# 96 free bytes behind the operand tile `tl`, and a DMA scratch of 1 KB, in a two-layer decoder trunk

## The chip, the core and the metric

The kernel runs on one core of one Trainium2 chip. The metric is the device time of one execution in microseconds. Besides TensorE (PE in the profile, its weight loads PEld) it uses VectorE (DVE), ScalarE (ACT), a little GpSimd (POOL), and SyncE (SP), whose queue issues all DMAs. On-chip memory (SBUF) is spoken of by a tile's address within one partition; all 128 partitions hold the same layout.

## What is computed

The reference is a decoder trunk of two layers over 256 tokens of width 1024, in float32, cut here to its frame:

```python
for layer in range(DEPTH):                       # DEPTH = 2
    x = x + mixer_block(rms_norm(x, nm), wi, wa, wb, wo)
    h = rms_norm(x, nf)
    x = x + (swiglu(h, *fp) if layer % 2 == 0 else moe_swiglu(h, *fp))
return rms_norm(x, norm_final)
```

`mixer_block` projects the 1024 columns to 5888 (queries, keys and values of two attentions, two gates), runs the attentions, projects each branch back to 1024, gates and adds them, and applies an output projection. `swiglu` is `(silu(h @ w_gate) * (h @ w_up)) @ w_down` with an inner width of 2816. `moe_swiglu` does the same with 8 experts of inner width 3584, two experts per token. The weights come to 429 blocks of 1 MiB.

## The kernel before

**Weights.** A `Stream` (lines 119 to 167) loads the weights in blocks of 128 x 2048 float32 into a ring of tiles: `raw0` to `raw3`, later also `ringa0` to `ringa5`, `ringb0` to `ringb3` and, once each, `late0` and `late1`. SP issues the load of a block when the block that lay in its slot has been split. Half a block at a time (128 x 1024) is split into two float32r parts: ACT copies it to a tile `wh` (line 152), DVE subtracts that from the original and writes a tile `wl` (line 153). `take()` keeps the split `AHEAD = 4` halves in front of the products, and `wh` and `wl` have five buffers each.

**Products.** Activations too are kept as two float32r parts, transposed, with 1024 rows spread over 128 partitions. `th` and `tl` hold the two parts of the normalised input of each stage (and of the merged branches ahead of the output projection); in the expert stage they hold the gathered tokens of an expert. `gTh` and `gTl` hold the inner activations of the dense channel mixer, `gT` and `tmp` those of the experts (two buffers that take turns; `tmp` also holds an expert's weighted result), and `oAh`, `oAl`, `oBh`, `oBl` the outputs of the two attentions. `run` (lines 250 to 260) multiplies: the activation part is the stationary operand (128 x 128, so 512 bytes of each partition), the weight part the moving operand (up to 512 columns, 2048 bytes of each partition). Three products make one: high by high (line 254), low by high (line 255), then high by low of the weights (line 259):

```python
for b, o in enumerate(outs):
    T.matmul(o, xh(b), wh, start=start, stop=False)
    T.matmul(o, xl(b), wh, start=False, stop=False)
...
    T.matmul(o, xh(b), wl, start=False, stop=stop)
```

In the first three stages (mixer, dense channel mixer, mixer) there are two outputs of 128 tokens, so half a block gives 12 products; in the experts there is one output, and half a block gives 6.

**Order.** The order of all work is written out by hand. `soon` and `later` put side work (transposes, softmax, gathers, scatters) between the products at distances counted in products, by `tick`. Each engine runs its instructions in that order and waits on semaphores.

**Where tiles lie.** Pools take SBUF in the order in which they are opened. At address 0 lies a scratch area for DMA descriptors, 16384 bytes unless the program says otherwise; the tiles of the pool `base` follow in the order of the code, each rounded up to 32 bytes: `xs`, `C`, `CB`, the four `raw`, `th`, `tl`, then `ss`, `ms`, `rstd`, `nhalf`, `base_e` (five of 32 bytes), `junk` (1024), `wrhl` (512) and `zeros` (256). Behind `base` lies the pool `hp` with `wh` and `wl`, and behind that the pools of the stages. Pools with `side="right"` (the attentions' work tiles, `ringa`) grow from the other end. `th` and `tl` (lines 210 and 211) start at 256 modulo 512, and the small tiles behind them shift all that follows by 416, so `wh`, `wl` and the tiles of the stages start at 160 modulo 512.

Of the kernel before, what the change touches and what calls it, by code (L numbers as in the profile page):

```python
# [11 lines left out]
F32 = mybir.dt.float32  # L12
# [3 lines left out]
AF = mybir.ActivationFunctionType  # L16
# [3 lines left out]
P = 128  # L20
# [15 lines left out]

# distances of the steps of the attention, the norms and the experts, in us of the weights' products
PAR = dict(a_step=4.02, a_e=1.5, a_n=4.0, a_t=8.7, a_v=11.7, a_act_n=0, a_act_t=1,
# [3 lines left out]

# [1 line left out]

# [59 lines left out]

# [1 line left out]
C_ID = 0  # L106
# [12 lines left out]
class Stream:  # L119
    """Weights in blocks of 1 MiB: loaded into a ring, then split exactly into two float32r parts, half a block at a time."""  # L120

# [49 lines left out]
def trunk(ctx: ExitStack, tc: tile.TileContext, x, xt, wpre, wmoe, cst, cstb, gfin, out):  # L171
    nc = tc.nc
# [18 lines left out]

# [1 line left out]
    xs = base.tile([P, 2, D], F32, name="xs")  # L193
# [16 lines left out]
    th = base.tile([P, 8, S], F32R, name="th")  # L210
    tl = base.tile([P, 8, S], F32R, name="tl")
    ss = base.tile([P, 2, 2], F32, name="ss")
    ms = base.tile([P, 2], F32, name="ms")
# [6 lines left out]

# [1 line left out]
    urgent, side = [], []  # L222
# [27 lines left out]
    def run(blocks):  # L250
        """Products with both parts of a block of weights: [(w_hi, w_lo, x_hi, x_lo, outs, start, stop)]."""
        for wh, wl, xh, xl, outs, start, stop in blocks:
            for b, o in enumerate(outs):
                T.matmul(o, xh(b), wh, start=start, stop=False)  # L254
                T.matmul(o, xl(b), wh, start=False, stop=False)  # L255
            tick(len(outs) * wh.shape[-1] / 1200)
        for wh, wl, xh, xl, outs, start, stop in blocks:
            for b, o in enumerate(outs):
                T.matmul(o, xh(b), wl, start=False, stop=stop)  # L259
            tick(len(outs) * wh.shape[-1] / 2400)  # L260
# [4 lines left out]
    def half(xT, outs, k0, nk, width, first, last):  # L265
        """Half a block of weights: row blocks k0.. of one chunk of columns."""
        h, l = W.take()
        r = []
        for i in range(nk):
            o = i * width  # L270
            r.append((h[:, o:o + width], l[:, o:o + width], col(xT[0], k0 + i), col(xT[1], k0 + i),
                      [p[:, 0:width] for p in outs], first and i == 0, last and i == nk - 1))
        run(r)
# [6 lines left out]
    def chunk(outs, xT=(th, tl), c=512, first=False):  # L280
        """One chunk of columns of a product over 1024 rows: two blocks of 512 columns, or one of 256."""
        if c == 512:
            unit(xT, outs, 0, 4, 512, True, False)
            if first:
                flush()
            unit(xT, outs, 4, 4, 512, False, True)
        else:
            unit(xT, outs, 0, 8, 256, True, True)

# [1 line left out]
    def gain(gi, k):  # L291
# [21 lines left out]
    def norm_half(gi, c):  # L313
        at = PAR['xt0'] if c == 0 else PAR['xt1']
        if gi == 3 and c == 1:
            # the router waits for it
            sumsq(xs, c)
        soon(at, lambda: x_transpose(gi, 2 * c))
        soon(at + 0.8, lambda: x_transpose(gi, 2 * c + 1))
        if gi != 3 or c == 0:  # L320
            soon(at + 1, lambda: sumsq(xs, c))
# [13 lines left out]

# [1 line left out]
    def mixer(i, gnext, last=False):  # L337
# [26 lines left out]
    def attention(mp, ap):  # L364
# [34 lines left out]
        def qk(src, kofs, pair, kind, mx):  # L399
            """Masked scores of two heads, in SBUF, with their row maxima."""  # L400
            s = [acc_ps(), acc_ps()]
            for b, (c0, c1) in enumerate(HALVES):
                for i in range(2):
                    h = slice(i * HD, (i + 1) * HD)
                    T.matmul(s[i][:, c0:c1], src[h, pair, b * P:(b + 1) * P], src[h, kofs + pair, 0:c1 - c0],
                             start=True, stop=True)
            prs = []
            for i in range(2):
                pr = ap.tile([P, 384], F32, name="pr", tag="pr", bufs=12)
                for b, (c0, c1) in enumerate(HALVES):  # L410
                    V.tensor_tensor_reduce(pr[:, c0:c1], s[i][:, c0:c1], mask[:, kind * 384 + c0:kind * 384 + c1],
                                           1.0, -3.0e38, ALU.add, ALU.max, mx[:, i, b:b + 1])
                prs.append(pr)
            return prs
# [24 lines left out]
        def weigh(items, dst, pair):  # L439
            """Weighted values, transposed: [(row offset of the head, transposed weights, values)]."""  # L440
            o = tp_ps()
            tot = len(items) // 2
            for n, (r, pt, v) in enumerate(items):
                T.matmul(o[r:r + HD, 0:S], v[:, 0, :], pt[:, 0:256], start=n < 2, stop=False,
                         skip_group_check=True)
            for n, (r, pt, v) in enumerate(items):
                T.matmul(o[r:r + HD, P:S], v[:, 1, :], pt[:, 256:384], start=False, stop=n // 2 == tot - 1,
                         skip_group_check=True)
            split_ps(dst[0][:, pair, :], dst[1][:, pair, :], o[:, 0:S])
# [78 lines left out]

        # queries and keys of A
        o = pair_ps()  # L530
# [9 lines left out]
        rope_chunk(o, qkA, 4)  # L540
        # values of A
        o = pair_ps()
# [4 lines left out]
        queue_A(PAR['a_step'])  # L547
        # queries and keys of B
        for c in range(3):
            o = pair_ps()  # L550
            chunk(o)
            rope_chunk(o, qkB, 4 * c)
        # values of B
        o = pair_ps()
# [8 lines left out]
        queue_B()  # L563
        # gates
        gates = []
# [14 lines left out]

    # projections of the branches, gated and summed
    def projections(mp, attended):
# [40 lines left out]

# [1 line left out]
    def ffn(gnext):  # L625
# [41 lines left out]

# [1 line left out]
    def more_slots(n, **kw):  # L669
# [8 lines left out]
    def moe_open():  # L678
        A.activation(junk[:, 0:2], nhalf, AF.Silu)     # its table, ahead of the experts
        ep = M["ep"] = ctx.enter_context(tc.tile_pool(name="moe", bufs=2, reuse_waits="tile"))  # L680
        # tiles of the experts' later steps, until then room for one more block each
        late = [ep.tile([P, UNIT], F32, name=f"late{i}", tag=f"late{i}", bufs=1) for i in range(2)]
        M["late"] = late
        W.add_slots(late, once=True)
        M["xo"] = late[1].rearrange("p (b d) -> p b d", b=2)
        M["gT"] = [ep.tile([P, 2, 4, P], F32R, name="gT", bufs=1)]
        more_slots(RING_MOE - RING_ATT, name="ringb")

    def logits(c):
        """The router's products with four of the eight row blocks."""  # L690
        if c == 0:
# [7 lines left out]
    def route():  # L699
# [16 lines left out]
        for b in range(2):  # L716
            V.scalar_tensor_tensor(L[:, b, :], lp[b][:, 0:8], rstd[:, b:b + 1], lo[:, b, :],
                                   op0=ALU.mult, op1=ALU.add)
        # rank by value, then by index
        lt = C[:, C_LT:C_LT + 64].rearrange("p (e j) -> p e j", e=8).unsqueeze(1).to_broadcast([P, 2, 8, 8])  # L720
# [8 lines left out]
        for b in range(2):  # L729
            V.tensor_copy(rc[:, b, :, 0], rstd[:, b:b + 1].to_broadcast([P, 8]))  # L730
        # slots are counted from 1, 0 where the expert is not chosen
        pp = mm_ps()
# [9 lines left out]
        def weights():  # L742
# [4 lines left out]
            for b in range(2):  # L747
                V.max(v8[:, b, :], L[:, b, :])
            # softmax of the two chosen: 1 / (1 + e^(m1 + m2 - 2 l))
            for b in range(2):  # L750
# [11 lines left out]
    def expert_prep(e, off):  # L762
        """The tokens of an expert's slots off..off+127: selection, gathered operand, their scales."""
        ep, par = M["ep"], e % 2
# [136 lines left out]
    def warm(n):  # L901
        """Products that nobody reads: they keep the tensor engine's clock up while it waits."""
        p = mm_ps()
# [40 lines left out]

# [1 line left out]
    most = nc.values_load(M["most"][0:1, 0:1], min_val=0, max_val=S)  # L946
# [6 lines left out]

# [1 line left out]
    xo = M["xo"]  # L955
# [9 lines left out]

# [1 line left out]
def constants(inputs):  # L967
# [60 lines left out]
```

## Time and profile before

| what | us |
|---|---|
| three timed runs | 1637.98, 1638.15, 1639.14 |
| their median | 1638.15 |
| the profiled execution, first to last instruction (its span) | 1637.1 |
| PE busy in it | 1620.4 |
| DVE busy | 1296.4 |
| ACT busy | 1096.2 |

The profiled execution has no separate time beside its span; the span lies 1.05 us below the median of the three runs.

The profile comes from one execution. A busy share says how long an engine had an instruction in work, not that it went at its best rate: products on PE are pipelined, their recorded durations overlap, and how fast they follow each other is read from the distance between their starts. The view of instructions in order of time gives these starts; the view of groups gives counts, busy time, mean duration and the idle time ahead of a group with what ended it. The stages by time: first mixer to 203 us, dense channel mixer to about 400 us, second mixer to 603 us, routing to about 615 us, experts to 1627 us, final norm.

### The profile page before, as it was taken

The page shows a single profiled execution, that of the slowest core. Times are in us where ns is not written, and L with a number is a line of the kernel's source. Part 1 is how long each engine was busy: PE and PEld are TensorE (multiplying, and loading weights), DVE is VectorE, ACT ScalarE, POOL GpSimd, SP SyncE. Part 2 cuts the span into 40 slices and gives each one's busy share as a digit, 9 for nine tenths or more (in the row PEclk, how much of TensorE's full clock was granted, in tenths as well). Part 3 has the DMA queues.
Part 4 walks back from the last instruction along what each step waited for, and adds up shares of the span by engine and source line. Part 5 has one row for each costly group of instructions (what it writes and reads, how often), then busy time and mean ns, then how long its engine had stood idle before and what let it go on. Part 6 is the DMA issues. An engine that isn't in the chain of part 4 may idle for free. (4 is left out here: it accounts for less than half of the span.)

```text
span 1637.1 us, 21105 instructions
## 1 busy us (share of the span) xinstructions
PE 1620.4 (99%) x7661; PEld 1308.2 (80%) x7661; DVE 1296.4 (79%) x1654; ACT 1096.2 (67%) x1413; POOL 6.6 (0%) x10
## 2 busy tenths in 40 slices
PE   9999999999999999999999999999999999999996
PEld 6777888888777778888888888888888888888885
DVE  7767655555776668899899889889889899889996
ACT  6556454445556447777777777777777777777774
POOL 0000000000000000000000000000000000000000
PEclk9999999999999999999999999999999999999998
DMA  8444545455444596899899999999999899989960
GB/s 328 163 146 139 179 171 188 176 189 203 165 144 147 215 385 232 332 362 348 334 358 360 335 361 346 337 365 346 333 374 346 335 362 357 356 327 369 349 255 28
DMA packets 64305, 456.17 MB, mean 279 GB/s; under 512 B 7104, under 2 KB 7360, under 8 KB 9408
## 3 DMA queue, kind: packets, MB, share of 16 engines
q1 hardware_dynamic: 64192, 454.73, 74.3%
q8 instruction: 62, 1.02, 0.2%
q14 instruction: 51, 0.42, 0.1%
HBM read 453.66 MB, written 1.05 MB: 278 GB/s over the span
## 5 line engine op out<-in xcount | busy, mean ns | idle before, releaser
L254 PE MATMUL mm<-wh,th 128*128 128x512 f32 (+1 forms) x1536 | 611.4, 400 | 2.0 <-ACT wh L152 2.0
L255 PE MATMUL mm<-wh,tl 128*128 128x512 f32 (+1 forms) x1536 | 599.1, 392 | 0.0
L153 DVE TENSOR_TENSOR wl<-raw,wh 128x1024 fp32r<-128x1024 f32 x376 | 448.3, 1220 | 142.1 <-ACT wh L152 141.2
L152 ACT ACTIVATE wh<-raw 128x1024 fp32r<-128x1024 f32 x376 | 390.9, 1058 | 154.6 <-PE mm L255 118.4
L259 PE MATMUL mm<-wl,th 128*128 128x512 f32 (+1 forms) x1536 | 459.2, 395 | 0.0
L153 DVE TENSOR_TENSOR wl<-ringa,wh 128x1024 fp32r<-128x1024 f32 x290 | 341.6, 1220 | 30.4 <-ACT wh L152 28.9
L254 PEld LDWEIGHTS mm<-wh,th 128*128 128x128 f32 x1536 | 289.9, 189 | 70.6 <-issue 5.0
L255 PEld LDWEIGHTS mm<-wh,tl 128*128 128x128 f32 x1536 | 290.2, 189 | 61.5
L259 PEld LDWEIGHTS mm<-wl,th 128*128 128x128 f32 x1536 | 281.5, 188 | 64.1 <-issue 2.0
L152 ACT ACTIVATE wh<-ringa 128x1024 fp32r<-128x1024 f32 x290 | 298.4, 1058 | 40.9 <-PE mm L255 24.4
L153 DVE TENSOR_TENSOR wl<-ringb,wh 128x1024 fp32r<-128x1024 f32 x188 | 219.0, 1220 | 21.5 <-ACT wh L152 21.4
L152 ACT ACTIVATE wh<-ringb 128x1024 fp32r<-128x1024 f32 x188 | 192.9, 1061 | 27.2 <-PE mm L255 12.7
L255 PE MATMUL acc<-wh,gT 128*128 128x512 f32 x224 | 87.5, 391 | 0.0
L254 PE MATMUL acc<-wh,gT 128*128 128x512 f32 x224 | 87.5, 391 | 0.0
L255 PE MATMUL acc<-wh,tmp 128*128 128x512 f32 x224 | 87.5, 391 | 0.0
L254 PE MATMUL acc<-wh,tmp 128*128 128x512 f32 x224 | 87.4, 390 | 0.0
L259 PE MATMUL acc<-wl,gT 128*128 128x512 f32 x224 | 69.2, 390 | 0.0
L259 PE MATMUL acc<-wl,tmp 128*128 128x512 f32 x224 | 69.2, 390 | 0.0
L865 ACT ACTIVATE g<-mm,sc 128x512 f32<-128x512 f32 x56 | 38.7, 692 | 42.2 <-PE mm L259 42.2
L254 PEld LDWEIGHTS acc<-wh,tmp 128*128 128x128 f32 x224 | 42.1, 188 | 9.0
L254 PEld LDWEIGHTS acc<-wh,gT 128*128 128x128 f32 x224 | 42.1, 188 | 9.0
L255 PEld LDWEIGHTS acc<-wh,gT 128*128 128x128 f32 x224 | 42.0, 188 | 9.1
(178 smaller groups left out, 1260.0 us busy)
## 6 DMA issues: line engine op xcount, KB each, us to landing
ringa<-in_wmoe_dram SPq DMA_DIRECT2D x144, 1024.0 KB, 6.7
raw<-in_wmoe_dram SPq DMA_DIRECT2D x96, 1024.0 KB, 6.4
ringb<-in_wmoe_dram SPq DMA_DIRECT2D x94, 1024.0 KB, 6.7
raw<-in_wpre_dram SPq DMA_DIRECT2D x91, 1024.0 KB, 4.8
late<-in_wmoe_dram SPq DMA_DIRECT2D x2, 1024.0 KB, 7.9
raw<-in_wpre_dram SPq DMA_DIRECT2D x2, 512.0 KB, 6.3
xs<-in_x_dram SPq DMA_DIRECT2D x2, 512.0 KB, 6.4
ringa<-in_wpre_dram SPq DMA_DIRECT2D x1, 1024.0 KB, 7.0
```

The source lines that it names most:

```text
L152: self.nc.scalar.activation(h, s, AF.Copy)
L153: self.nc.vector.tensor_tensor(l, s, h.bitcast(F32), op=ALU.subtract)
L254: T.matmul(o, xh(b), wh, start=start, stop=False)
L255: T.matmul(o, xl(b), wh, start=False, stop=False)
L259: T.matmul(o, xh(b), wl, start=False, stop=stop)
L865: A.activation(g, og, AF.Silu, scale=sl["sc"][:, 0:1])
```

## The change

96 bytes are taken in the pool `base` behind `tl`, by a tile `gap` that nothing reads or writes, and the program is built with a DMA scratch of 1024 bytes in place of 16384. The diff also drops comments, which is left out here.

```diff
     th = base.tile([P, 8, S], F32R, name="th")
     tl = base.tile([P, 8, S], F32R, name="tl")
+
+    base.tile([P, 24], F32, name="gap")
     ss = base.tile([P, 2, 2], F32, name="ss")
...
-    nc = bacc.Bacc("TRN2", target_bir_lowering=False, num_devices=1)
+    nc = bacc.Bacc("TRN2", target_bir_lowering=False, num_devices=1, dynamic_dma_scratch_size=1024)
```

In the built programs the instructions of every engine stand in the same order with the same waits; nothing but addresses differs. The scratch moves all tiles on the left side down by 15360 bytes, which is 30 times 512. The start addresses modulo 512:

| tiles | before | after |
|---|---|---|
| `th`, `tl` | 256 | 256 |
| `wh`, `wl` (all ten buffers) | 160 | 256 |
| `gTh`, `gTl`, `gT`, `tmp`, `oAh`, `oAl`, `oBh`, `oBl` | 160 | 256 |
| `raw0` to `raw3` | 256 | 256 |
| `ringa0` to `ringa5` | 480 | 480 |
| `ringb0` to `ringb3` | 384 | 480 |
| `late0`, `late1` | 160 | 256 |
| `xs`, the identity in `C` | 128 | 128 |
| `G` (selection of an expert's tokens) | 352 | 448 |
| `GT` (the same, transposed) | 384 | 480 |
| `g` in the dense stage, in the experts | 160, 320 | 256, 416 |
| `merged0`, `merged1`, `t1`, `qkA`, `vA`, gates | 160 | 256 |
| `pr`, `pt`, `qkB`, `vB` | 96 | 96 |

The rows of `th` and of the other operand tiles are multiples of 512 bytes long, so each stationary operand starts at its tile's place modulo 512, and each moving operand of 512 columns too.

## Rows read from the trace of the kernel before

**Rows 1.** The page: span; busy us of each engine; granted TensorE clock in 40 slices.
```profile
span 1637.1 us, 21105 instructions
...
PE 1620.4 (99%) x7661; PEld 1308.2 (80%) x7661; DVE 1296.4 (79%) x1654; ACT 1096.2 (67%) x1413; POOL 6.6 (0%) x10
...
PEclk9999999999999999999999999999999999999998
```

**Rows 2.** Waits of PE, longest first: waiting, releaser, us, times, longest us.
```profile
PE mm L254 <- ACT wh L152: 2.0, 2, 1.7
```

**Rows 3.** Groups by shape: line, engine, operation, names, shapes, count, busy us, mean ns.
```profile
L254 PE MATMUL mm<-wh,th 128*128 128x512 f32 x1472 | 595.9, 405 | 2.0 <-ACT wh L152 2.0
L255 PE MATMUL mm<-wh,tl 128*128 128x512 f32 x1472 | 583.6, 396 | 0.0
L259 PE MATMUL mm<-wl,th 128*128 128x512 f32 x1472 | 450.1, 399 | 0.0
...
L255 PE MATMUL acc<-wh,gT 128*128 128x512 f32 x224 | 87.5, 391 | 0.0
...
L255 PE MATMUL mm<-wh,gTl 128*128 128x512 f32 x88 | 34.3, 390 | 0.0
...
L254 PE MATMUL mm<-wh,th 128*128 128x256 f32 x64 | 15.6, 282 | 0.0
...
L255 PE MATMUL mm<-wh,oAl 128*128 128x512 f32 x32 | 12.5, 391 | 0.0
```

**Rows 4.** PE in order of time, dense stage, gate products: start us, us, instruction.
```profile
253.72 0.40 PE L254 MATMUL mm<-wh,th 128*128 128x512 f32 x1
...
262.16 0.60 PE L632 MATMUL tp<-C,g 128*128 128x128 f32 x4
```

**Rows 5.** The same view, dense stage, down projection.
```profile
375.64 0.40 PE L254 MATMUL mm<-wh,gTh 128*128 128x512 f32 x1
...
383.81 0.39 PE L254 MATMUL mm<-wh,gTh 128*128 128x512 f32 x1
```

**Rows 6.** The same view, first mixer, output projection.
```profile
194.92 0.39 PE L254 MATMUL mm<-wh,th 128*128 128x512 f32 x1
...
200.54 0.39 PE L254 MATMUL mm<-wh,th 128*128 128x512 f32 x1
```

**Rows 7.** The same view, experts: an up chunk, then the down projection.
```profile
1030.94 0.39 PE L254 MATMUL mm<-wh,th 128*128 128x512 f32 x1
...
1036.55 0.39 PE L254 MATMUL acc<-wh,gT 128*128 128x512 f32 x1
...
1042.02 0.60 PE L882 MATMUL tp<-C,g 128*128 128x128 f32 x4
1042.38 0.48 PE L254 MATMUL mm<-wh,th 128*128 128x512 f32 x1
1042.70 0.40 PE L255 MATMUL mm<-wh,tl 128*128 128x512 f32 x1
```

**Rows 8.** Busy us in stretches of 50 us; at the end clock, DMA share, GB/s.
```profile
1000.00:1050.00 50.00, 49.98 (x231) 40.73 (x230) 46.12 (x47) 37.28 (x43) 0.00 (x0) 1.00 0.96 352
```

**Rows 9.** Instructions writing `wl`: duration ns min/median/max, first and last start us.
```profile
L153 DVE TENSOR_TENSOR wl<-raw,wh x376: 1210/1219/1228, 7.2 to 1607.9; 128x1024 fp32r<-128x1024 f32 x188
...
L153 DVE TENSOR_TENSOR wl<-late,wh x4: 1217/1218/1219, 642.0 to 645.4; 128x1024 fp32r<-128x1024 f32 x4
```

**Rows 10.** DMA: GB/s in 40 slices, queues, issues with us to landing.
```profile
GB/s 328 163 146 139 179 171 188 176 189 203 165 144 147 215 385 232 332 362 348 334 358 360 335 361 346 337 365 346 333 374 346 335 362 357 356 327 369 349 255 28
...
q1 hardware_dynamic: 64192, 454.73, 74.3%
...
ringa<-in_wmoe_dram SPq DMA_DIRECT2D x144, 1024.0 KB, 6.7
...
ringb<-in_wmoe_dram SPq DMA_DIRECT2D x94, 1024.0 KB, 6.7
```

**Rows 11.** Waits of the SP queue: waiting, releaser, us, times, longest us.
```profile
SPq L142 <- DVE wl L153: 1289.7, 392, 19.3
```

## The prediction, made before the changed kernel ran

> **What bounds the kernel now.** [...] Then the waits: the longest wait of PE in total is 2.0 us, for ACT's `wh` [rows 2]. So PE never waits for a feeder, and what PE's instructions take one behind the other is the time. DVE is busy 46.12 of 50 us in a stretch of the experts, second to PE but with 3.9 us to spare [rows 8]; SP's queue spends 1289.7 us waiting for DVE to free a ring slot [rows 11], so the loads wait for the products and not the other way round.
>
> A busy share of 99% doesn't say that the products go at their best rate. So the third view is PE in order of time, and there the distance between starts. The dense stage gives two stretches of 36 products, three half blocks of 12, with no other instruction between them:
> - gate products, `th` and `tl` stationary: from 253.72 to 262.16 us, 8.44 us, 234.4 ns each [rows 4];
> - down projection, `gTh` and `gTl` stationary: from 375.64 to 383.81 us, 8.17 us, 226.9 ns each [rows 5].
>
> Same shapes, types, moving tiles and PSUM tiles (`mm`), and a difference of 7.5 ns. The experts show it back to back: 24 products with `th` from 1030.94 to 1036.55 us, 233.8 ns each, then 24 with `gT` to 1042.02 us, 227.9 ns each [rows 7]. The mean durations agree: 396 to 405 ns with `th` and `tl`, 390 or 391 ns with `gT`, `gTl` and `oAl` [rows 3]. It isn't the data: in the output projection `th` holds the merged branches instead of a norm's output, and 24 products from 194.92 to 200.54 us take 234.2 ns each [rows 6]. Nor is it the stage, since each of them holds both kinds. What the 234 ns products have in common, and none of the 227 ns products shares, is the place: `th` and `tl` start at 256 modulo 512 and meet weights at 160, while `gT`, `gTl`, `oAl` and their kin start at 160, as the weights do.
>
> **The change, part by part.** No instruction is added, removed or moved, and no wait. What changes is where `wh` and `wl` lie: at 256, the place of `th` and `tl`. The other stationary tiles go along to 256, so every product with weights then has both operands at one place, as the 227 ns products have today.
>
> *The products with `th` and `tl`.* There are 3 x 1472 = 4416 of 512 columns [rows 3]. In the experts they are 8 experts x 14 chunks x 8 row blocks x 3 = 2688, so 1728 lie in the first three stages. I take for each kind the difference in its own stage: 1728 x 7.5 ns = 13.0 us, and 2688 x (233.8 - 227.9 = 5.9 ns) = 15.9 us. Together 28.9 us. All of this is on the path, since PE waits for nothing. By the smaller difference for all it is 26.1 us, by the larger 33.1 us.
>
> *The 192 products of 256 columns* (3 x 64 [rows 3]) have no counterpart at one place in the trace. Between nothing and half of the 7.5 ns each they are worth 0 to 0.7 us; I take 0.3, as half the columns stream by.
>
> *Products just behind other work on PE.* Behind transposes the first product takes 0.32 us to the next start [rows 7], 85 ns above the usual, because its weights can't be loaded ahead. Such a product may gain nothing. By the order in the code there are some 200 (each group of transposes, gathers or scores makes one), so 0 to 1.5 us of the 28.9 would fail to come; I take 0.8.
>
> *The products with the other stationary tiles* number 3 x (224 + 224 + 88 + 32 + 16) = 1752, for `gT`, `tmp`, `gTh`, `oAh` and `oBh` (three of these counts, or those of the twin product, stand in [rows 3]). Both their operands move by 96 together. If only the distance between them matters, they stay at 227 to 228 ns. If the place itself matters they could go to 234 ns, 7.5 x 1752 = 13.1 us lost at the most, or win something that no row prices. I take 0: the nearest rows are these products themselves, at an unchanged distance.
>
> *Small products.* Transposes take 0.60 us for four with the source at 160 (`g` of the dense stage [rows 4]) and 0.60 us with it at 320 (`g` of the experts [rows 7]) against the same identity, so places don't show there. The gathers, scores and weighted values, some 500 products of 128 to 256 columns, change their distances too; at a quarter of 7.5 ns each way that is 1 us up or down. I take 0.
>
> *ACT and DVE* read and write the same tiles at new places: `wl`, `wh` and `raw` then lie at one place. The four splits from `late` already have that, all three at 160, and take 1218 ns against 1219 ns where `raw` lies 96 away [rows 9]. No price, and it is off the path by the margin above.
>
> *DMA.* `ringb` goes from 384 to 480, where `ringa` is; both land 6.7 us behind their issue [rows 10]. The smaller scratch has no reader: all loads go through the hardware queue, 64192 packets [rows 10], and POOL issues none. If it delayed a load after all, the loads wait on free slots far ahead of the products [rows 11]. The products will ask for more: 15.9 us less in the experts' 985 us is 1.6%, some 358 GB/s in place of 352 [rows 8], while a slice of 41 us ran at 385 [rows 10].
>
> The sum: 28.9 + 0.3 - 0.8 = 28.4 us off the profiled execution's 1637.1, so a span of 1608.7; with the 1.05 us by which the median lies above that span, **1609.8 us**. Its own range is 25 to 33 us less, to which I add the 1 us of the small products: 1604 to 1614.
>
> **Rivals.**
>
> *The place of the stationary tile itself decides, not its distance to the weights (slower).* The trace can't refute this: every 227 ns product has its stationary at 160, every 234 ns one at 256, and all weights lie at 160. If starting at 256 is what costs, `th` and `tl` keep their 234 ns and the 1752 others join them: 1752 x 5.9 to 7.5 ns = 10.3 to 13.1 us more, **about 1650 us**. It decides as soon as a stationary at 256 is slow against weights at 256. Against it: 256 is a rounder place than 160, and a cost for the rounder one, with nothing else to meet there, is hard to see; two reads that run at the same time and get in each other's way by their distance is the simpler picture. Chance 0.09.
>
> *Nothing to gain.* The two groups might differ by something else about the tiles (their region of SBUF, say), and the places follow by accident: **1638 us**. For it speaks that `th` and `tl` lie below the weights and the fast tiles above them, before and after the change. Against it: the 234 ns products go through six row blocks of `th` and `tl` at one pace [rows 4] and through four at the same pace [rows 6], and the 227 ns products are as even over six row blocks of `gTh` and `gTl` [rows 5]; a matter of regions would hardly be so flat. [...] Chance 0.07.
>
> *Another engine takes over.* DVE is at 46.12 of 50 us in the experts [rows 8]; with 1.6% less time it comes to 46.9, and in the denser parts of an expert (gather, scatter) its results could come late for PE. If half of the experts' gain went this way it is 8 us: 1618; if all of it, **1626 us**. For it: DVE's share. Against it: the split runs four halves ahead, and PE's waits are 2.0 us today [rows 2]. Chance 0.06.
>
> *More than forecast.* If 227 ns too is the price of an odd place (160) and 256 serves better, all 6168 products gain further; 1 to 2 ns each would give 6 to 12 us more, about 1600. No row shows it. Chance 0.03.
>
> That the change doesn't do what it says is no rival: the built program has the tiles at these addresses.
>
> **How the numbers follow.** Forecast 0.75, another engine 0.06, more 0.03, nothing 0.07, slower 0.09. The forecast's own range of 1604 to 1614 I hold good for nine in ten of its cases (0.69). With the other engine's cases up to 1626 (0.06) and most of the "more" case down to 1598 (0.02), and the forecast's tails, that is some 0.82: the range is 1598 to 1627. About 0.2% (3.3 us) is what a measurement of this kernel can tell from no change. Faster by more than that: 0.75 + 0.06 + 0.03 = 0.84; within it 0.07; slower by more 0.09.
>
> **What would show it.** In the order of time, 36 gate products of the dense stage should span 8.17 us, not 8.44, and the 24 expert products with `th` 5.47, not 5.61; the down projections should keep 8.17 and 5.47. The mean durations of lines 254, 255 and 259 with `th` and `tl` should fall to the 390 of the others. PE's waits should stay near 2 us. If the down projections rise to 8.44 with the gates unchanged, the stationary's own place was the cause; if both stay, neither was. If the products come closer but waits for `wh`, `wl` or `tmp` open up on PE, another engine took over. The forecast is wrong too if DVE's split of 1219 ns gets longer.

## The result and the profile after

| kernel | median, us | lowest to highest | runs |
|---|---|---|---|
| before | 1638.27 | 1637.98 to 1639.14 | 4 |
| after | 1613.67 | 1613.32 to 1614.59 | 4 |

The ratio is 0.9852, with a 95% interval of 0.9838 to 0.9866: 24.6 us less, against 28.4 forecast. The time lies in the range of 1598 to 1627 and inside the forecast's own 1604 to 1614, at its upper end. The profiled execution of after has a time of 1613.7 us and a span of 1611.9, so 1.8 us lie around the span, where the forecast had taken 1.05; of the span 25.2 us are gone.

In the code of after all lines behind `tl` stand two further down: 254, 255 and 259 of before are 256, 257 and 261. The page of after, in the parts that [rows 1] shows of before:

```profile
span 1611.9 us, 21105 instructions
...
PE 1593.9 (99%) x7661; PEld 1306.4 (81%) x7661; DVE 1293.2 (80%) x1654; ACT 1096.8 (68%) x1413; POOL 6.6 (0%) x10
...
PEclk9999999999999999999999999999999999999998
```

PE's busy time fell by 26.5 us with the same 7661 instructions, while the other engines' hardly moved; the granted clock is at 0.9 or above in the same 39 slices. So the bulk of the gain isn't the clock's (one short stretch, in the routing, is; it comes below); the products follow each other more closely. The groups by shape (line, engine, operation, names, shapes, count, then busy us and mean ns of one, then idle us ahead) say which ones, against [rows 3]:

```profile
L256 PE MATMUL mm<-wh,th 128*128 128x512 f32 x1472 | 588.6, 400 | 2.0 <-ACT wh L152 2.0
L257 PE MATMUL mm<-wh,tl 128*128 128x512 f32 x1472 | 576.6, 392 | 0.0
L261 PE MATMUL mm<-wl,th 128*128 128x512 f32 x1472 | 442.3, 395 | 0.0
...
L257 PE MATMUL acc<-wh,gT 128*128 128x512 f32 x224 | 87.3, 390 | 0.0
...
L256 PE MATMUL mm<-wh,th 128*128 128x256 f32 x64 | 15.8, 285 | 0.0
```

The three groups with `th` and `tl` went from 405, 396 and 399 to 400, 392 and 395 ns; `gT` from 391 to 390. They didn't come down all the way to 390: that is where the missing part will be found. The products of 256 columns went up, from 282 to 285.

How fast products follow each other stands in the view in order of time (start us, us, instruction). The gate products of the dense stage, against [rows 4]:

```profile
246.62 0.39 PE L256 MATMUL mm<-wh,th 128*128 128x512 f32 x1
...
254.78 0.39 PE L256 MATMUL mm<-wh,th 128*128 128x512 f32 x1
```

36 products in 8.16 us, 226.7 ns each, where [rows 4] had 234.4. The down projection of the same stage, against [rows 5]:

```profile
369.53 0.39 PE L256 MATMUL mm<-wh,gTh 128*128 128x512 f32 x1
...
377.69 0.39 PE L256 MATMUL mm<-wh,gTh 128*128 128x512 f32 x1
```

Again 36 products in 8.16 us: unchanged, and now the same as the gates. The output projection of the first mixer, where [rows 6] had 234.2 ns:

```profile
192.07 0.39 PE L256 MATMUL mm<-wh,th 128*128 128x512 f32 x1
...
197.51 0.39 PE L256 MATMUL mm<-wh,th 128*128 128x512 f32 x1
```

24 products in 5.44 us, 226.7 ns each. And an expert, 24 products with `th` and `tl`, 24 with `gT`, then four transposes and the products behind them, against [rows 7]:

```profile
1014.54 0.39 PE L256 MATMUL mm<-wh,th 128*128 128x512 f32 x1
...
1019.98 0.39 PE L256 MATMUL acc<-wh,gT 128*128 128x512 f32 x1
...
1025.43 0.60 PE L884 MATMUL tp<-C,g 128*128 128x128 f32 x4
1025.78 0.48 PE L256 MATMUL mm<-wh,th 128*128 128x512 f32 x1
1026.10 0.40 PE L257 MATMUL mm<-wh,tl 128*128 128x512 f32 x1
...
1028.64 0.39 PE L256 MATMUL mm<-wh,th 128*128 128x512 f32 x1
```

5.44 us for the first 24 (226.7 ns, was 233.8), 5.45 us for the next 24 (227.1 ns, was 227.9). Behind the transposes the first product takes 0.32 us as in [rows 7], and the eleven after it, from 1026.10 to 1028.64, take 230.9 ns each: they don't reach 226.7 at once.

The longest two waits of PE (what waits, its releaser, total us, times, longest us), against [rows 2]:

```profile
PE mm L256 <- ACT wh L152: 2.0, 1, 2.0
PE tp L842 <- DVE tmp L835: 1.9, 8, 0.3
```

The second was 0.3 us in one place before: a scatter's products now come upon DVE's result too early eight times, 1.9 us in all. A stretch of the experts (length, then busy us and instructions of PE, PEld, DVE, ACT and POOL; clock, DMA share, GB/s), against [rows 8]:

```profile
1000.00:1050.00 50.00, 50.00 (x246) 41.95 (x245) 44.35 (x50) 38.59 (x48) 0.00 (x0) 1.00 0.90 343
```

PE has no gap, DVE still has 5.6 us to spare. The exact split on DVE, against [rows 9]:

```profile
L153 DVE TENSOR_TENSOR wl<-raw,wh x376: 1207/1220/1227, 7.0 to 1583.0; 128x1024 fp32r<-128x1024 f32 x188
```

The median duration of the split is 1220 ns, was 1219, now that `raw`, `wh` and `wl` start at one place. SP's queue waits 1266.7 us for DVE, was 1289.7 [rows 11]: the loads still wait for the products.

### The profile page after: what moved, and what is told of

The parts are those of the page before. It is cut to its first block, busy times and chain, and to the rows that moved or that the text cites. A ratio compares the mean times of both kernels' runs of the same rounds, so it can differ in the third digit from the quotient of the medians.

```text
span 1611.9 us, 21105 instructions
## 1 busy us (share of the span) xinstructions
PE 1593.9 (99%) x7661; PEld 1306.4 (81%) x7661; DVE 1293.2 (80%) x1654; ACT 1096.8 (68%) x1413; POOL 6.6 (0%) x10
## 3 DMA queue, kind: packets, MB, share of 16 engines
q8 instruction: 62, 1.02, 0.2%
HBM read 453.66 MB, written 1.05 MB: 282 GB/s over the span
## 5 line engine op out<-in xcount | busy, mean ns | idle before, releaser
L256 PE MATMUL mm<-wh,th 128*128 128x512 f32 (+1 forms) x1536 | 604.3, 395 | 2.0 <-ACT wh L152 2.0
L257 PE MATMUL mm<-wh,tl 128*128 128x512 f32 (+1 forms) x1536 | 592.3, 387 | 0.0
L261 PE MATMUL mm<-wl,th 128*128 128x512 f32 (+1 forms) x1536 | 451.5, 390 | 0.0
L153 DVE TENSOR_TENSOR wl<-ringa,wh 128x1024 fp32r<-128x1024 f32 x290 | 340.5, 1220 | 27.9 <-ACT wh L152 27.8
L153 DVE TENSOR_TENSOR wl<-ringb,wh 128x1024 fp32r<-128x1024 f32 x188 | 217.7, 1220 | 19.4 <-ACT wh L152 19.4
L261 PEld LDWEIGHTS acc<-wl,gT 128*128 128x128 f32 x224 | 42.1, 188 | 8.8
L257 PEld LDWEIGHTS acc<-wh,gT 128*128 128x128 f32 x224 | 42.1, 188 | 8.8
```

What stands on the lines that cost most here:

```text
L153: self.nc.vector.tensor_tensor(l, s, h.bitcast(F32), op=ALU.subtract)
```

## Where the 25.2 us lie

From the starts of all products in both traces I took the distance to the next start of each product of 512 columns with `th` or `tl`, by stage and by how many such products stand between it and the last other work on PE (transposes, scores, gathers). In the second table a product counts only where the next instruction on PE is again a product with weights, so its counts come to 4263 and not to 4416.

| stage | gain of the span, us | forecast, us |
|---|---|---|
| first mixer (624 of these products) | 3.1 | 4.7 |
| dense stage (480) | 3.0 | 3.6 |
| second mixer (624) | 2.7 | 4.7 |
| routing (none) | 1.5 | 0 |
| experts (2688) | 14.7 | 15.9 |

(The forecast of a stage is its count times 7.5 ns, 5.9 ns in the experts, as the prediction had it. The remaining 0.2 us lie at the start and the end.)

The 1.5 us of the routing aren't the change's. Between the small products of the router stand ten bf16 products on a tile of zeros, whose results nothing reads. Before, then after (start us, us, instruction), and the stretch around them in each (length, busy us as above, then clock, DMA share, GB/s):

```profile
608.14 3.79 PE L905 MATMUL mm<-zeros 128*128 128x512 bf16 x10
605.00:610.00 5.00, 4.63 (x23) 3.04 (x22) 3.23 (x12) 1.43 (x5) 0.70 (x1) 0.77 1.02 426
```

```profile
599.09 2.33 PE L907 MATMUL mm<-zeros 128*128 128x512 bf16 x10
595.00:600.00 5.00, 4.63 (x31) 3.33 (x30) 2.35 (x8) 2.58 (x8) 0.70 (x1) 1.00 1.03 429
```

In the profiled execution of before the granted clock fell to 0.50 there, the value of each microsecond from 608 to 611; in that of after it is 1.00 in each from 599 to 602. The fall is no property of the change: in the profiled execution of the last experiment below, whose operands of the products with weights lie as in after, the same ten take 4.02 us. So the change itself is worth some 23.7 us of the span in this pair of traces. The timed runs agree: where the span and the granted clock of an execution are on record and the clock's mean is 0.996, the span averages 1636.5 us for before (14 executions) and 1612.4 us for the kernels whose tiles lie 0 or 256 apart (12), which is 24.1 us less.

| place of a product of `th` or `tl` behind other work on PE | products | before, ns | after, ns |
|---|---|---|---|
| first | 208 | 315.3 | 313.9 |
| second to tenth | 1350 | 234.6 | 232.2 |
| eleventh and further | 2705 | 234.4 | 226.8 |

The products that run undisturbed win 7.6 ns, the prediction's 7.5. The first one wins next to nothing, as it said. But the nine behind it win 2.4 instead of 7.6. That is an observation over two traces; whether the break causes it is tried below.

## Experiments

Two theories stood at the start. **Distance**: what counts is how far the stationary and the moving operand of a product lie apart, modulo some period. **Own place** (the prediction's slower rival, turned round): what counts is where one of the tiles lies by itself. Beside them stood **nothing of the gap**: the DMA scratch, which moves all tiles on the left side by 15360 bytes, or the region, does it.

### One part at a time

The gap alone, with the scratch of 16 KB:

```diff
-    nc = bacc.Bacc("TRN2", target_bir_lowering=False, num_devices=1, dynamic_dma_scratch_size=1024)
+    nc = bacc.Bacc("TRN2", target_bir_lowering=False, num_devices=1)
```

> The 96 bytes behind tl, with the DMA scratch left at 16 KB, so that all tiles have the same places modulo 512 as in the changed kernel, 15360 bytes higher. Distance theory (stationary and moving operand at one place modulo 512 is what gains): 1613 to 1614 us, the products with th and tl 228 to 229 ns apart. Scratch theory (the smaller scratch or the lower region of SBUF had a share): up to 1638 us.

Measured: 1614.19 us (1613.44 to 1615.71), ratio to before 0.9849 (0.9833 to 0.9866), as after. The first group of this kernel:

```profile
L256 PE MATMUL mm<-wh,th 128*128 128x512 f32 x1472 | 588.3, 400 | 2.2 <-ACT wh L152 2.2
```

The scratch of 1 KB alone:

```diff
-    base.tile([P, 24], F32, name="gap")
```

> The DMA scratch of 1 KB without the 96 bytes: th and tl at 256, weights at 160 modulo 512, as before, 15360 bytes lower. Distance theory: 1638 us, 234 ns between the starts of products with th and tl. Scratch or region theory: some of the 24.6 us gained, 1614 to 1630 us.

Measured: 1638.19 us, ratio 0.9994 (0.9985 to 1.0004): as before. Its first group:

```profile
L255 PE MATMUL mm<-wh,th 128*128 128x512 f32 x1472 | 594.8, 404 | 2.3 <-ACT wh L152 2.3
```

So the gap is the whole of the gain, and the scratch is worth nothing that can be measured here.

### `th` at the place of the fast tiles, but 96 bytes from the weights

Free bytes are put ahead of `th` in place of behind `tl`, so many that `th` and `tl` start at 160, where every fast stationary tile lay before, while the weights and the other stationary tiles lie at 64. Own place says that `th` is fast here, distance says that it isn't:

```diff
+    base.tile([P, 104], F32, name="gap")
     th = base.tile([P, 8, S], F32R, name="th")
     tl = base.tile([P, 8, S], F32R, name="tl")
-
-    base.tile([P, 24], F32, name="gap")
```

> Scratch of 1 KB, and 416 free bytes ahead of th instead of 96 behind tl: th and tl at 160 modulo 512, weights and the other stationary tiles at 64, so th and tl keep the distance of 96 that they had before, but stand where gT and its kin stood. Distance theory: 1638 us, 234 ns with th and tl, 227 ns with gT and gTh. Own-place theory (a stationary at 160 is quick, one at 256 is not): th and tl at 227 ns, 1610 us or less, and gT, now at 64, anywhere.

Measured: 1638.06 us, ratio 0.9994 (0.9985 to 1.0004). Its groups:

```profile
L256 PE MATMUL mm<-wh,th 128*128 128x512 f32 x1472 | 595.8, 405 | 1.6 <-ACT wh L152 1.6
...
L257 PE MATMUL acc<-wh,gT 128*128 128x512 f32 x224 | 87.5, 391 | 0.0
```

`th` stays at 405 at 160, `gT` stays at 391 at 64. Own place has fallen, and the region of SBUF with it: `th` lies below the weights here as it does in the fast kernels, and free bytes that leave the distance at 96 change nothing.

### The other stationary tiles put 96 bytes off

The counter-trial inside the kernel: the gap stays, and the tiles of the later pools (`gT`, `tmp`, `gTh`, `oAh` and their kin, 1752 products) go to 352, with the weights and `th` at 256.

```diff
+    off = ctx.enter_context(tc.tile_pool(name="off", bufs=1))
+    off.tile([P, 24], F32, name="gap2")
```

> The changed kernel with 96 more free bytes between wl and the tiles of the stages: th, tl, wh and wl stay at 256, while gTh, gTl, gT, tmp and the attentions' outputs go to 352. Distance theory: the products with th and tl keep their 228 ns, the 1752 others go from 227.5 to about 234 ns, 1752 x 6 to 7 ns = 10.5 to 12.3 us more than the changed kernel: 1624 to 1626 us. If the gain belonged to th and tl alone, whatever their distance: 1614 us.

Measured: 1624.81 us, ratio 0.9922 (0.9905 to 0.9938); 11.1 us over after. Its groups (line numbers two higher still):

```profile
L258 PE MATMUL mm<-wh,th 128*128 128x512 f32 x1472 | 587.0, 399 | 2.5 <-ACT wh L152 2.5
...
L259 PE MATMUL acc<-wh,gT 128*128 128x512 f32 x224 | 88.8, 396 | 0.0
```

`gT` went from 390 to 396 ns, while `th` kept its gain. 11.1 us over 1752 products is 6.4 ns each, between the 5.9 and 7.5 ns from which the prediction's slower rival was priced. The price is that of the distance, whichever tile pays it.

### All distances, without the kernel

A kernel of its own leaves the trunk out: it runs 48 products of 128 x 128 by 128 x 512 per group into one PSUM bank, with the moving operand `mv` at one place and the stationary `st` at another, and nothing else on the core, except in two groups that have copies on ACT and DVE beside them, on tiles of their own (`traffic`). It was executed once, and so was the second kernel of this kind further down.

```python
def group(name, m, s, src=(mv, st), n=N, nst=8, each=None):
    p = ps.tile([P, 512], F32, name=name, tag="p", bufs=4)
    for k in range(n):
        mo, so = m + 512 * (k // 2 % 8), s + 128 * (k % nst)
        T.matmul(p, src[1][:, so:so + 128], src[0][:, mo:mo + 512], start=k == 0, stop=k == n - 1)
```

> Not the trunk: only products of 128x128 by 128x512 float32r in groups of 48, nothing else beside them, each group with its own places of the moving and stationary operand modulo 512 (atM st S in the names of the groups; the output is only x copied). Distance theory: 227 ns at equal places whatever the place (0, 96, 160, 256), about 234 ns at a distance of 96 either way of the same sign, and some curve over the 16 distances of 32 bytes. Own-place theory: the time follows the stationary's place alone, and the groups with the stationary at 0 take the same whatever the moving operand's place. If it is a conflict with ACT and DVE rather than between PE's two reads, the sweep is flat and only the two groups with copies on ACT and DVE beside them differ.

PE in order of time (start us, us of the whole group, then the group, whose name says at which byte `mv` and `st` start; the time of a group is the distance to the next start):

```profile
32.30 11.05 PE L48 MATMUL at0st0x<-mv,st 128*128 128x512 f32 x48
43.19 11.35 PE L48 MATMUL at0st32x<-mv,st 128*128 128x512 f32 x48
...
65.58 11.40 PE L48 MATMUL at0st96x<-mv,st 128*128 128x512 f32 x48
76.82 11.32 PE L48 MATMUL at0st128x<-mv,st 128*128 128x512 f32 x48
...
121.37 11.05 PE L48 MATMUL at0st256x<-mv,st 128*128 128x512 f32 x48
132.26 11.35 PE L48 MATMUL at0st288x<-mv,st 128*128 128x512 f32 x48
...
266.19 11.08 PE L48 MATMUL at96st96x<-mv,st 128*128 128x512 f32 x48
277.11 11.09 PE L48 MATMUL at160st160x<-mv,st 128*128 128x512 f32 x48
...
332.39 21.95 PE L48 MATMUL traffic0x<-mv,st 128*128 128x512 f32 x96
354.18 22.65 PE L48 MATMUL traffic96x<-mv,st 128*128 128x512 f32 x96
376.67 10.53 PE L48 MATMUL half0x<-mvb,stb 128*128 128x512 bf16 x48
387.04 10.52 PE L48 MATMUL half64x<-mvb,stb 128*128 128x512 bf16 x48
```

From start to start, a product takes:

| distance of the two starts, bytes | ns |
|---|---|
| 0 (both at 0, at 96, at 160, at 256) | 226.9, 227.5, 227.5, 227.9 |
| 256 | 226.9 |
| 4, 8, 16 | 232.3, 230.6, 233.3 |
| 32, 64, 96 | 233.1, 233.3, 234.2 |
| 128, 160, 192, 224 | 232.5, 233.3, 229.2, 233.1 |
| 288 to 480 in steps of 32 | as at 32 to 224 |
| `st` at 0, `mv` at 32, 96, 160, 256, 416 | 233.3, 233.3, 234.0, 226.7, 234.2 |
| 0 and 96 with copies on ACT and DVE | 227.0, 234.3 |
| 0 and 96 again, behind the bf16 groups | 231.7, 234.2 |
| bf16 in place of float32r: 0, 64, 96 | 216.0, 215.8, 215.8 |

The kernel's 226.7 and 234.4 are these numbers, from two tiles alone. At every distance that was tried the period is 256 bytes, not 512, whichever of the two tiles moves. Four bytes cost 5.4 ns already, so this is no matter of alignment to some size: of the starts that were tried, those equal modulo 256 run at 226.7 to 227.9 ns (but for the repetition behind the bf16 groups), the others at 229.2 or more. Copies on other engines change nothing (227.0 and 234.3 ns beside them, 226.9 and 234.2 without). That leaves PE's own two reads, the running product's and the next weights', as what gets in each other's way: PE and PEld are busy at the same time, 50.00 and 41.95 us of the 50 us above. This is argued from what is left; no run shows it directly.

The spread within distance 0, and the 231.7 of its repetition, come from the start of a group. From the eleventh product on all five groups run at 226.6 or 226.7 ns; the first ten of the slower ones take 224 to 236, and the first product behind the bf16 groups 418.

For bf16 no effect of the distance shows: 216.0, 215.8 and 215.8 ns at 0, 64 and 96. For float32r the places do matter: 226.9 ns at the best distance and 229 to 234 at the others. Whether the type itself is the reason stays open, since the loads differ too: a weight load takes 98 ns in the bf16 groups and 188 in those of float32r, and the same in after (a median of 98 for the products on `zeros`, a mean of 188 with `th`).

### A distance of 256 in the kernel

If the period is 256, 352 free bytes must do as well as 96; the weights then lie at 0, `th` at 256.

```diff
-    base.tile([P, 24], F32, name="gap")
+    base.tile([P, 88], F32, name="gap")
```

> The changed kernel with 352 free bytes behind tl instead of 96: th and tl stay at 256, weights and the other stationary tiles go to 0 modulo 512, so the distance is 256 and not 0. By the sweep, in which the starts lie 226.9 ns apart at distances 0 and 256 alike, only the place modulo 256 counts: 1613 to 1615 us. If it takes one place modulo 512, as the change has it: 1638 us.

Measured: 1614.02 us, ratio 0.9852 (0.9835 to 0.9868). The kernel's change speaks of 512; 256 is enough.

### Why the products behind other work win less

After a break the next nine products gain 2.4 ns, not 7.6. Two causes were possible: the break itself (float32 transposes, behind which the weights of the first product are loaded late: in after the load starts 25 to 28 ns ahead of it behind the 56 groups of transposes of `g` in the experts, against 230 ns ahead of the second to the tenth product behind any break, in the median), or ACT and DVE reading PSUM, which is what they do at those places. A second kernel of its own, again without the trunk, runs sets of 16 products at distance 0 and at 96: in one unbroken row (`clean`), behind four transposes (`behind`), beside reads of PSUM without transposes (`read`), with both (`both`), and sets of four behind transposes (`four`).

```python
for q in range(sets):
    if breaks:
        for i in range(4):
            T.transpose(b[:, i * P:(i + 1) * P], raw[:, i * P:(i + 1) * P], ident)
    elif read:
        T.matmul(b, st[:, s:s + 128], mv[:, 0:512], start=True, stop=True)
    if read:
        reads(b)
    for k in range(n):
        ...
```

> Not the trunk: float32r products of 128x128 by 128x512 at distances 0 and 96, in sets of 16 (or of 4), alone, behind four transposes each, beside a read of PSUM by ACT and DVE, or both; the output is only x copied. Question: why products with th and tl stay at 228.4 ns on the average when gT has 227.1. Break theory: behind four transposes not the first product alone but a dozen lose, so a set of 16 takes over 16 x 226.9 + 85 ns = 3.72 us at distance 0, the surplus being smaller at 96. Read theory: it is ACT's and DVE's reading of PSUM, then the sets behind transposes without reads take 3.72 us and those beside reads without transposes more than 3.63 us.

PE in order of time, a set of three of the kinds at 0 and then at 96:

```profile
46.97 29.18 PE L58 MATMUL clean0x<-mv,st 128*128 128x512 f32 x128
75.99 0.60 PE L50 MATMUL tp<-ident,raw 128*128 128x128 f32 x4
76.34 3.92 PE L58 MATMUL behind0x<-mv,st 128*128 128x512 f32 x16
80.10 0.60 PE L50 MATMUL tp<-ident,raw 128*128 128x128 f32 x4
...
109.09 3.79 PE L58 MATMUL read0x<-mv,st 128*128 128x512 f32 x16
112.71 0.39 PE L53 MATMUL rd<-mv,st 128*128 128x512 f32 x1
...
172.57 30.15 PE L58 MATMUL clean96x<-mv,st 128*128 128x512 f32 x128
202.56 0.60 PE L50 MATMUL tp<-ident,raw 128*128 128x128 f32 x4
202.91 3.98 PE L58 MATMUL behind96x<-mv,st 128*128 128x512 f32 x16
206.73 0.60 PE L50 MATMUL tp<-ident,raw 128*128 128x128 f32 x4
...
236.19 3.91 PE L58 MATMUL read96x<-mv,st 128*128 128x512 f32 x16
239.93 0.40 PE L53 MATMUL rd<-mv,st 128*128 128x512 f32 x1
```

| 16 products | at 0, us | at 96, us | gain, us |
|---|---|---|---|
| unbroken (an eighth of 128) | 3.63 | 3.75 | 0.12 |
| beside reads of PSUM | 3.62 | 3.74 | 0.12 |
| behind four transposes | 3.76 | 3.82 | 0.06 |
| both | 3.76 | 3.82 | 0.06 |
| (four products behind four transposes) | 1.01 | 1.02 | 0.01 |

Reads of PSUM cost nothing (3.62 us beside them, 3.63 without); the break halves the gain, from 0.12 to 0.06 us. Behind it the first product at distance 0 takes 316 ns to the next start (means of the eight sets), the second to the tenth 228 to 235, and from the eleventh on 226 to 227. These are the classes found in the kernel, and the second to the tenth gain 2.5 ns here, 2.4 there: in the kernel the break is the cause. It isn't the only thing that does it, however. In the sweep the group with both tiles at 160 follows the one with both at 96, with no other work between, and its first ten products take 224 to 236 ns as well, in much the same order as behind transposes, before it runs at 227. Not every change does it: the groups with `mv` at 0 and `st` at 256, and the other way round, are at 227 from their first product on. So what is lost is the even pace, and where it is lost some ten products pass until it is back. Why so many, when in after the weights of the second are already loaded 232 ns ahead (median) and those of the eleventh 228, the runs don't say.

### Could the rest be had?

Two small things in after invited a try: the 1.9 us that the scatter's products wait for DVE, and `GT`, which lies at 480 while the tiles that it meets lie elsewhere. The scatter is put 0.6 us later, and 32 bytes are put ahead of `GT`:

```diff
-           s0=1.2, sd0=0.6, s1=2.6, sd1=1.5, gt=5.0, gl=2.4, p1=4.0, p2=6.0, p3=8.0, p4=9.0, q3=0.6, q4=9.0)
+           s0=1.8, sd0=0.6, s1=2.6, sd1=1.5, gt=5.0, gl=2.4, p1=4.0, p2=6.0, p3=8.0, p4=9.0, q3=0.6, q4=9.0)
...
+            small([P, 8], "gap3")
```

> The changed kernel with the experts' first scatter put off by 0.6 us of products (s0 from 1.2 to 1.8) and 32 free bytes ahead of GT, so that GT and tmp lie at one place modulo 256. In the changed kernel the scatters waited for DVE's low part in tmp 7.6 us in all, 1.5 us more on PE than before. If these waits stand on PE's path: 1.5 to 5 us less than the changed kernel, 1609 to 1612 us. If they are covered, the same 1613 to 1614 us.

Measured: 1618.02 us (1617.73 to 1619.88), 4.3 us slower than after, where 1.5 to 5 us less or no change had been expected. Its waits of PE:

```profile
PE tp L885 <- DVE late L845: 7.7, 7, 1.1
...
PE tp L843 <- DVE tmp L836: 0.4, 1, 0.4
```

The wait that was aimed at shrank to 0.4 us, and a larger one came up behind it: the next transposes of `g` need the PSUM tile that DVE's sums of the scatter free, and these sums now come later, 7.7 us in seven places. With the 32 bytes alone:

```diff
+            small([P, 8], "gap3")
```

> The run before had two edits; here the 32 free bytes ahead of GT alone, with s0 back at 1.2. If the delay cost that run its 4.3 us, this one is at the changed kernel's 1613 to 1614 us, 64 products with GT being some 6 ns closer each (0.4 us, too little to measure), and no wait of the transposes for DVE's sums in late. If the 32 bytes cost it (ringb then lies at 0 modulo 512): 1617 to 1618 us again.

1613.39 us (1612.85 to 1615.74), ratio to before 0.9849 (0.9835 to 0.9862), not to be told from after. So the delay cost the 4.3 us, and the place of `GT` is worth nothing measurable. No version tried is measurably better than after.

## Why the prediction was right, point by point

- **What bounds the kernel.** Right: PE's products, one behind the other, and the two levels of 234 and 227 ns. PE's time fell with every other engine's nearly unchanged, and the total went with it. The granted clock was read in slices of 41 us, which hid the fall to 0.50 for some 3 us in the routing.
- **Cause.** Right: the distance of the two operands; how it acts inside PE is not shown. Own place at 0.09 and nothing at 0.07 were refuted separately, the one by `th` at 160 that stayed at 405 ns, the other by the gap alone at 1614.19 us. The traces of before could not have told own place from distance; the experiment that keeps the distance and moves the place could.
- **The 4416 products.** The size of the step was right where nothing interrupts: 7.5 ns forecast, 7.6 measured over 2705 products. In the dense stage 3.0 of 3.6 us came, in the mixers 5.8 of 9.4, in the experts 14.7 of 15.9.
- **Products just behind other work on PE: the term that was mis-sized.** I took 0.8 us, for some 200 first products without a gain. There are 208, but the next nine behind each break lose most of it too: 1350 products at 2.4 instead of 7.6 ns is 7.0 us. The stretch that I read of before was chosen because nothing interrupts it, and was then taken for all 1728 products of the first three stages; a mean over the stage was needed, and the prediction's other row, the product behind the transposes, showed the break only at its first product.
- **Why that cost only 3.2 us of the span.** In the experts I used 5.9 ns, from one stretch of 24 products of each kind. Undisturbed, the step there is 7.1 (233.8 to 226.7). The smaller number was too small for the undisturbed products and so happened to be about right for all: over the experts the mean (without the distances above 260 ns) went from 233.9 to 228.2 ns, 5.7 less. Two errors met there, which is luck. Even so 4.2 us failed to come in the mixers and the dense stage and 1.2 in the experts, 5.4 together, against the 0.8 booked. With the smaller terms (the 0.3 of the next point, and 0.2 at the start and the end) the change fell 4.7 us short of the forecast span. That only 3.2 are missing is luck too: 1.5 us came from the clock in the routing.
- **Products of 256 columns.** Wrong in sign: 282 to 285 ns in duration, 1.6 ns more in distance, 0.3 us lost for 192 products, where I had taken 0.3 gained. I had bounded it by nothing from below. Why equal places don't help them wasn't tried.
- **The 1752 others.** Taken at 0. In the experts they went from 228.9 to 228.0 ns, 1.2 us gained, unexpected and within the 14.7; in the first three stages they stayed.
- **ACT, DVE, DMA.** No price, as forecast: the split took 1220 ns for 1219. Loads land 6.1 us behind their issue, was 6.7 [rows 10], off the path. (The experts run for 1009 us before, not 985; the 1.6% stand.)
- **Another engine takes over.** It did so in one small place: PE's waits for DVE's result at the scatter went from 0.3 to 1.9 us, which is why the experts stay below their 15.9 in spite of the 1.2 us. The rival's place was right and its price, 8 to 16 us, wasn't. The later scatter shows that it is near, however: 0.6 us of delay there costs 4.3.
- **More than forecast.** Refuted by the kernel of its own: with both operands at 0, 96, 160 or 256 the products run at 226.6 or 226.7 ns from the eleventh on; no place is better than 160 was by 1 to 2 ns.
- **Around the span.** Of the 3.8 us that are missing in the median (28.4 against 24.6), 3.2 lie in the span. The rest lies around it, 1.8 against the 1.05 that I had taken, which set the median of some executions against the span of another. In every execution whose time and span are both on record, 1.7 to 1.9 us lie between them.

## What to carry to other kernels

Where float32r products run one behind the other, let the stationary and the moving tile start at the same byte modulo 256, by a few free bytes in the pool; here it was 1.5% of the whole for 96 bytes, 226.8 ns in place of 234.4 for a product that runs undisturbed. A PE that is busy 99% can still lose time: compare the distances between starts of products of one shape in different places of the program, and if they fall into two levels, ask what the operands of each have in common. Count such a gain in full only for products that stand further than ten behind the last other work on PE (7.6 ns each here, 2.4 for the second to the tenth), and take the mean of a stage, not of its cleanest stretch. Read the clock over short stretches, too, before a gain is put down to a change; here some 3 us at 0.50 made 1.5 us of the difference.

## What the hardware showed that was not expected

- The period is 256 bytes, and every other distance tried costs, four bytes too: 226.9 ns at 0 and 256, 229.2 to 234.3 elsewhere, for 512 columns of float32r, at a granted clock of 1.00. The cheapest of the others is 192, at 229.2.
- The distance doesn't matter to bf16 products: 216.0 ns at 0, 215.8 at 64 and at 96. So a float32r product takes 11 ns longer than a bf16 one even at its best place.
- Behind four float32 transposes it takes ten products until the pace is back at 227 ns, and in some groups of the sweep nine or ten behind a mere change of place; four products behind a break are as long at 96 as at 0 (1.02 against 1.01 us).
